# One encoder layer on one core: earlier copies of an inverse, a second bank for local products, and more planned room between a product and what it waits for

## The chip, the cores and the metric

The kernel runs on one core of a Trainium2 chip. The metric is the device time of one execution in microseconds: the median of the runs shown, and beside it one execution recorded by the hardware profiler. All times are in microseconds (us) unless marked ns.

## The reference

One layer over a prompt of 2048 tokens and a sample of 32, 1024 wide, in fp32. What matters here is the order of the stages and the chunked delta rule of mixer B.

```python
h = rmsnorm(x) * (1 + sc1) + sh1
p = h @ w_in                                  # u, v | q, k, v | z | a, b
a_out = u * (W_s @ rmsnorm(v) + b_s)          # mixer A, chunks of 128 tokens
q, k, v = l2norm(silu(causal_conv(qkv)))      # mixer B, 4 heads of 128
sol = triangular_solve(I + tril(k k^T * decay), [v * beta, k * beta * exp(gc)])
for chunk: v_new = u_i - w_i @ s
           o = qg_i @ s + attn_i @ v_new
           s = s * gl_i + kg_i^T @ v_new
x = x + gt1 * (concat(a_out, b_out) @ w_out)
h = rmsnorm(x) * (1 + sc2) + sh2
y = rmsnorm(x + gt2 * (relu(h @ w_up)^2 @ w_down))
```

## The kernel before

**Stages.** The 2080 tokens go through the mixers in two halves (`hf` 0 and 1), each in groups of 512, 384 or 288 tokens. The stages on TensorE (PE) are: `startup` (L658: the first modulation columns, the norm, and the z columns of the first group), `v_stage` (L949: mixer A's v, 260 columns a tile), the q, k, v and z columns (L882 `mixers`, L1057 `qkv_tile`), `u_stage` (L1354), `out_stage` (L1368), and then the feed-forward part (L1532) to the end. A large product is three passes with a split of each operand into a high and a low part (`BH`, `BL` and `wh`, `wl`), 8 slices of 128 deep: 24 matmul instructions fill one PSUM bank of tag `g`. The feed-forward part names its banks `f`.

**Small products beside them.** Per head and half: *local* products per pair of 128-token chunks (`delta_local`, L1094: four transposes, two products of 256 columns and two transposes, all in the bank with tag `L`), an *inverse* of a 128 x 128 triangle per chunk (`delta_inv`, L1176), and a *chain* over the chunks (`delta_chain`, L1268): per chunk and pair of heads a step of four products with the state (`pa`), a step of two with the inverse (`px`), and a step of four (`pu`), all in banks of tag `C`. Each step reads what VectorE (DVE) or ScalarE (ACT) made of the step before. Other tags are `B` (the inverse) and `M` (norms).

**The inverse.** For each head, `delta_inv` cuts 16 x 16 diagonal blocks out of `nb` and copies them to a DRAM tile `nd` with eight copies (ten in the second half), reads `nd` back as `N` with one block a partition, solves on GpSimd (POOL), writes the result to `ud_d` with two copies (four in the second half) and reads it back as `ud`. All copies are issued by SyncE's queue (SP).

**What sets the order.** Nothing runs in the order of the text. `Program.op` records each operation with its engine, an assumed duration and its predecessors. Predecessors come from the regions that operations read and write (`Mem.read`, `Mem.write`). A `View` keeps the region it had before a `re` (a rearranged view): an index taken after `re` narrows the shape, not the region. `schedule` (L245) then lays all operations out in assumed time, and each engine's program is the order of their assumed starts. At run time every engine goes through its own list strictly in that order.

In `schedule` a priority goes first (CHAIN, INV, LOCAL, EVAC, GEMM; the large products are GEMM), except that on PE small operations may be held back: while a large product is also ready, a small one is not taken until `hold` ns after it became ready (L60: `HOLD`, for LOCAL alone, 1000). An operation becomes ready when each predecessor has ended, plus an assumed latency between the engines (L272). A `bank` (L463) is taken from the ring of its tag; the next user of a bank comes after the last reader of the one before.

Of the kernel before, what the change touches and what calls it, by code (L numbers as in the profile page):

```python
# [43 lines left out]
PE, DVE, ACT, POOL, DMA, NONE = range(6)  # L44
# [5 lines left out]
LATENCY = {(PE, DVE): 230, (PE, ACT): 230, (PE, POOL): 230, (DVE, PE): 380, (DVE, DVE): 130, (DVE, ACT): 160,  # L50
           (DVE, POOL): 190, (DVE, DMA): 150, (ACT, PE): 370, (ACT, DVE): 175, (ACT, ACT): 180, (ACT, POOL): 210,
           (ACT, DMA): 150, (POOL, PE): 390, (POOL, DVE): 100, (POOL, ACT): 130, (POOL, POOL): 130, (POOL, DMA): 100}
# [4 lines left out]

CHAIN, INV, LOCAL, EVAC, GEMM, IDLE = range(6)
TURN = 84
HOLD = {LOCAL: 1000}  # L60

# [143 lines left out]
class Program:  # L207
# [37 lines left out]
    def schedule(self):  # L245

        ops = self.ops
        due = [i if o.eng == PE and o.prio == GEMM else len(ops) for i, o in enumerate(ops)]
        for i in reversed(range(len(ops))):
            due[i] = min([due[i]] + [due[j] for j in ops[i].succ])  # L250
        key = [(o.prio, due[i] if o.prio >= EVAC else i, i) for i, o in enumerate(ops)]
        free = [0.0] * 6
        port = [0.0] * 6
        wait = [[] for _ in range(6)]
        ready = [([], []) for _ in range(6)]
        table, grid, large = None, (P, P), True
        order = []

        def release(i, t):
            o = ops[i]  # L260
            if o.eng == NONE:
                finish(i, t, t)
            else:
                heapq.heappush(wait[o.eng], (t, i))

        def finish(i, start, end):
            o = ops[i]
            o.start = start
            order.append((start, i))
            for j in o.succ:  # L270
                s = ops[j]
                s.ready = max(s.ready, end + o.lat + LATENCY.get((o.eng, s.eng), 0.0))  # L272
                s.npred -= 1
                if s.npred == 0:
                    release(j, s.ready)

        for i, o in enumerate(ops):
            if o.npred == 0 and o.start == 0.0 and o.eng != NONE:
                heapq.heappush(wait[o.eng], (0.0, i))
        for i, o in enumerate(ops):  # L280
            if o.npred == 0 and o.eng == NONE and not any(k == i for _, k in order[-1:]):
                finish(i, 0.0, 0.0)
                o.npred = -1

        other = {DVE: POOL, POOL: DVE}
        while True:
            best = None
            for e in range(5):
                shared = port[other[e]] - PORT if e in other else 0.0
                t = None  # L290
                if ready[e][0]:
                    t = free[e]
                elif ready[e][1]:
                    t = max(free[e], shared)
                if wait[e]:
                    at, i = wait[e][0]
                    at = max(free[e], at, shared if ops[i].port else 0.0)
                    t = at if t is None else min(t, at)
                if t is not None and (best is None or t < best[0]):
                    best = (t, e)  # L300
            if best is None:
                break
            t, e = best
            while wait[e] and wait[e][0][0] <= t:
                i = heapq.heappop(wait[e])[1]
                heapq.heappush(ready[e][ops[i].port if e != PE else ops[i].prio == GEMM], key[i])
            shared = port[other[e]] - PORT if e in other else 0.0
            tops = [q for q in (ready[e][0], ready[e][1] if shared <= t else None) if q]
            if not tops:
                continue  # L310
            top = min(tops, key=lambda q: q[0])
            if e == PE and large and len(tops) == 2 and all(t < ops[q[-1]].ready + ops[q[-1]].hold for q in tops[0]):
                top = tops[1]
            i = heapq.heappop(top)[-1]
            o = ops[i]
            end = t + o.cost
            if e == PE:
                if o.table and o.table != grid:
                    end += 110 if o.table == (P, P) else 95
                    grid = o.table  # L320
                elif o.prio == GEMM and not large:
                    end += TURN
                large = o.prio == GEMM
            elif o.table and o.table != table:
                end += 1280
                table = o.table
            free[e] = end
            if o.port:
                port[e] = end
            finish(i, t, end)  # L330
        assert len(order) == len(ops), (len(order), len(ops))
        self.span = max(free)
        order.sort()
        return [ops[i] for _, i in order]


class Kern:
# [211 lines left out]
    def setup(self):  # L549
# [14 lines left out]
        self.nslab, self.sn = 0, None  # L564
        self.slots = [{"m": Mem(SLOT), "t": None} for _ in range(NSLOT)]
        self.bmem = [Mem(512, whole=True) for _ in range(8)]
        self.banks = {"g": [0, 1, 2], "L": [3], "C": [4, 5], "B": [6], "M": [7]}
        self.rings, self.rshape = {}, {}
        for s in range(NSLOT):
            self.era(s, F32)  # L570
# [87 lines left out]
    def startup(self):  # L658
        i, c = self.i, self.dma
        c(self.craw, i["cT"])  # L660
        self.act(self.cs, self.craw, AF.Silu)
        self.fill(self.ones, 1.0, DVE)
        self.fill(self.mhalf, -0.5, DVE)
        xr = [[8, 9, 10, 11], [4, 5, 7, 12]]
        x = [[self.slot(s, lo, (P, 512)) for s in xr[g] for lo in (0, HALF)] for g in range(2)]
        load = lambda g: [c(x[g][k], self.x_src(0)(k, 512 * g, 512)) for k in range(KT)]
        row = [self.row[:, 512 * g : 512 * g + 512] for g in range(2)]

        def stats(g):
            acc = row[g]  # L670
            self.act(acc, x[g][0], AF.Square)
            for k in range(1, KT):
                sq = self.half("E")
                self.act(sq, x[g][k], AF.Square)
                self.tt(acc, acc, sq, ALU.add, DVE if g == 0 or k % 2 else POOL)
            self.rms_row([acc], 512, acc)

        load(0)
        k1 = self.slot(13, 512, (P, 248))
        c(k1, i["k1"])  # L680
        self.adab = k1[:, :96].re("p (j k q) -> p j k q", j=6, k=KT)
        self.cp(self.nrm, k1[:, 96:120].re("p (n k) -> p n k", n=3))
        self.cp(self.ident, k1[:, 120:248])
        stats(0)
        self.sq = self.slab_list()
        self.sn = self.slab(*self.sq.pop(0))
        z = [self.next_slab(), self.sn]
        ps = [self.bank("C") for _ in range(2)]
        for e in range(2):
            self.fill(ps[e], 0.0, DVE)  # L690
        zs = [self.bank(t) for t in "gggL"]
        for k in range(KT):
            self.ada_first(k, ps[k % 2])
            self.h_tile(0, 0, k, x[0][k], row[0], self.a1, 0)
            for h in range(H):
                self.gemm_k(zs[h][:, :512], *z[h // 2], h % 2, 0, 0, k)
        for h in range(H):
            self.z_out(0, 0, h, zs[h])
        load(1)
        stats(1)  # L700
        for k in range(KT):
            self.h_tile(0, 1, k, x[1][k], row[1], self.a1, 0)
        self.next_slab()
        self.consts()
# [471 lines left out]
    def delta_inv(self, hf, h, nb):  # L1176
# [4 lines left out]
        N, U, tmp = self.new("N")[:nblk], self.new("U")[:nblk], self.new("tmp")[:nblk]  # L1181
        M = nb[:, :1024].re("p (c i) -> p c i", c=8)
        nd = self.nd_d[h][hf]
        n16 = nd[:64].re("(s c a) (j i) -> s a j c i", s=2, c=8, j=16)
        for s in range(2):
            for a in range(4):
                d = slice(32 * a + 16 * s, 32 * a + 16 * s + 16)
                self.dma(n16[s, a], M[d, :, d])
            if hf == 1:
                d = slice(1024 + 16 * s, 1040 + 16 * s)  # L1190
                self.dma(nd[64 + s].re("(j i) -> j i", j=16), nb[16 * s : 16 * s + 16, d])
# [3 lines left out]
        Uv = U.re("p (j i) -> p j i", j=16)  # L1195
# [5 lines left out]
        ud_d = self.ud_d[self.nud % 2]  # L1201
        self.nud += 1
        for s in range(2):
            d = ud_d[:8].re("c a (s j t i) -> s t (c a) j i", s=2, j=16, t=2)
            self.dma(d[s, s], Uv[32 * s : 32 * s + 32])
            if hf == 1:
                d = ud_d[8:9, 0:1].re("c a (s j t i) -> s t (c a) j i", s=2, j=16, t=2)
                self.dma(d[s, s], Uv[64 + s : 65 + s])
        ud, td = self.new("ud"), self.new("td")
        self.dma(ud[:, :nch], ud_d[:nch].re("c a (j i) -> (a j) c i", j=32))  # L1210
        tr = lambda: self.transpose32(td[:, :nch].re("p c i -> p (c i)"), ud[:, :nch].re("p c i -> p (c i)"))
# [445 lines left out]
    def put(self, ops, name, m, x):  # L1657
        ops.setdefault(name, {})[m] = self.operand(self.rp, x)
# [238 lines left out]
```

## Time and profile before

| | |
|---|---|
| median of 3 runs (lowest to highest) | 2337.24 (2336.88 to 2339.47) |
| the profiled execution | 2330.84 |
| its span, first to last instruction | 2328.8 |
| DVE busy | 1653.2 (71%) |
| ACT busy | 1226.1 (53%) |
| POOL busy | 607.5 (26%) |
| granted TensorE clock, mean | 0.998 |

The profiled execution is 6.4 below the median of the runs, and 2.0 above its own span. Busy shares are averages over stages with different limits. A matmul's record is longer than the time until the next one starts, since matmuls are pipelined: with 512 columns a record lasts about 0.39 and the next starts 0.23 later. So how late a matmul is can be seen from the distance of two starts, and only partly from the idle time that the profile gives.

### The profile page before, as it was taken

Reading aid. Unit: us, or ns where it says so; the run is one execution under the profiler, and the core shown is the slowest. Engines: PE = TensorE matmul, PEld = TensorE weight load, DVE = VectorE, ACT = ScalarE, POOL = GpSimd, SP = SyncE. Lnnn points to the kernel's source line nnn. Section 1 sums busy time; section 2 is a strip of 40 time slices with the busy share of each in tenths; the row PEclk is TensorE's granted clock in tenths of the full one; section 3 lists DMA queues with packets and bytes.
Section 4 is the critical chain, followed back from the end, with each engine's and each line's share of the span. In section 5 each row is a group of like instructions: output and inputs, shape, how many; then the busy total and the mean of one; then the engine's idle time right before and its main releaser. Section 6 shows DMA issues by size and latency. Waiting matters only on the chain.

```text
span 2328.8 us, 45703 instructions
## 1 busy us (share of the span) xinstructions
PE 2292.2 (98%) x15906; PEld 2171.0 (93%) x15906; DVE 1653.2 (71%) x3651; ACT 1226.1 (53%) x2816; POOL 607.5 (26%) x830
## 2 busy tenths in 40 slices
PE   7999999999999999999999999999999999999998
PEld 4877879999999888999999999999999999999998
DVE  5557646667655546589999989776668886666775
ACT  5465546666655435376556555753344564334343
POOL 2235331332423323345544424200000250000001
PEclk9999999999999999999999999999999999999999
DMA  9789666657557767888777786997667797666771
GB/s 322 224 291 317 222 183 214 188 166 232 165 157 225 242 204 232 262 290 277 248 255 251 256 280 229 344 321 233 221 214 252 264 302 232 221 214 215 246 225 54
DMA packets 367247, 552.59 MB, mean 237 GB/s; under 512 B 70988, under 2 KB 191200, under 8 KB 367016
## 3 DMA queue, kind: packets, MB, share of 16 engines
q1 hardware_dynamic: 367016, 549.68, 72.5%
q8 instruction: 125, 2.05, 0.4%
q14 instruction: 106, 0.87, 0.1%
HBM read 395.25 MB, written 154.28 MB: 236 GB/s over the span
## 4 chain that ended last, share of the span: by engine, by line
PE 59%; DMA 3%; DVE 2%; issue 1%; ACT 1%; POOL 0%; SPq 0%; POOLq 0%; DVEq 0%; ACTq 0%
PE f L412 52%; PE g L412 6%; DMA s<-th_d 1%; PE C L412 1%; DVE s L366 1%; DVE s L371 1%; ACT s L351 0%; DVE BL L366 0%; DMA wh<-sd_d 0%; DVE wl L366 0%; POOL s L366 0%; DMA wr<-w_o 0%; PE B L412 0%; DMA th_d<-s 0%; ACT BH L351 0%
## 5 line engine op out<-in xcount | busy, mean ns | idle before, releaser
L351 ACT ACTIVATE s<-s 128x348 fp32r<-128x348 f32 (+13 forms) x1077 | 496.0, 483 | 341.3 <-DVE s L366 131.4
L412 PE MATMUL f<-s,wh 128*128 128x348 f32 (+1 forms) x2768 | 662.4, 322 | 0.4 <-DVE s L366 0.3
L412 PEld LDWEIGHTS f<-s,wh 128*128 128x128 f32 x2768 | 481.0, 188 | 2.2 <-DVE s L366 1.9
L366 DVE TENSOR_TENSOR s<-f,s 128x348 f32<-128x348 f32 (+1 forms) x696 | 349.6, 515 | 170.4 <-PE f L412 169.2
L412 PE MATMUL f<-s,wl 128*128 128x348 f32 (+1 forms) x1384 | 444.9, 321 | 0.0
L412 PE MATMUL g<-BH,wh 128*128 128x512 f32 (+2 forms) x1112 | 411.3, 370 | 0.0
L412 PE MATMUL g<-BH,wl 128*128 128x512 f32 (+2 forms) x1112 | 391.4, 352 | 0.0
L412 PE MATMUL g<-BL,wh 128*128 128x512 f32 (+2 forms) x1112 | 390.1, 351 | 0.0
L366 DVE TENSOR_TENSOR s<-s,s 128x348 fp32r<-128x348 f32 (+7 forms) x679 | 350.9, 546 | 45.7 <-POOL s L366 16.7
L412 PE MATMUL f<-BL,wh 128*128 128x348 f32 (+1 forms) x1024 | 330.2, 322 | 0.0
L412 PE MATMUL f<-BH,wh 128*128 128x348 f32 (+1 forms) x1024 | 329.3, 322 | 0.0
L412 PE MATMUL f<-BH,wl 128*128 128x348 f32 (+1 forms) x1024 | 328.7, 321 | 0.0
L351 ACT ACTIVATE wh<-s 128x512 fp32r<-128x512 f32 (+1 forms) x277 | 173.7, 634 | 232.0 <-PE f L412 190.6
L366 POOL TENSOR_TENSOR s<-s,s 128x512 f32<-128x512 f32 (+5 forms) x156 | 197.6, 1275 | 330.5 <-ACT s L351 163.4
L366 POOL TENSOR_TENSOR s<-s 64x39 f32<-64x39 f32 (+12 forms) x298 | 159.5, 535 | 444.0 <-issue 381.7
L412 PEld LDWEIGHTS f<-s,wl 128*128 128x128 f32 x1384 | 260.6, 188 | 0.0
L366 DVE TENSOR_TENSOR wl<-s,wh 128x512 fp32r<-128x512 f32 (+1 forms) x277 | 215.4, 786 | 35.7 <-ACT wh L351 34.6
L412 PEld LDWEIGHTS g<-BH,wh 128*128 128x128 f32 x1112 | 209.6, 188 | 22.7 <-issue 5.2
L412 PEld LDWEIGHTS g<-BH,wl 128*128 128x128 f32 x1112 | 208.9, 188 | 19.1
L412 PEld LDWEIGHTS g<-BL,wh 128*128 128x128 f32 x1112 | 210.0, 189 | 16.7 <-DVE BL L366 0.2
L371 DVE SCALAR_TENSOR_TENSOR s<-s,s,s 128x256 f32<-128x256 f32 (+5 forms) x318 | 164.2, 538 | 59.4 <-ACT s L351 34.2
L366 DVE TENSOR_TENSOR wl<-wr,wh 128x512 fp32r<-128x512 f32 (+2 forms) x164 | 159.1, 973 | 57.5 <-ACT wh L351 54.9
(116 smaller groups left out, 3328.0 us busy)
## 6 DMA issues: line engine op xcount, KB each, us to landing
s<-w_u SPq DMA_DIRECT2D x124, 256.0 KB
s<-w_d SPq DMA_DIRECT2D x121, 256.0 KB
wh<-su_d SPq DMA_DIRECT2D x114, 256.0 KB
wl<-su_d SPq DMA_DIRECT2D x114, 256.0 KB
wh<-sd_d SPq DMA_DIRECT2D x100, 256.0 KB
wl<-sd_d SPq DMA_DIRECT2D x100, 256.0 KB
wr<-w_b SPq DMA_DIRECT2D x42, 512.0 KB
s<-adaw SPq DMA_DIRECT2D x32, 512.0 KB
```

The source lines that it names most:

```text
L351: self.p.op(ACT, c, lambda: nc.scalar.activation(out=R(out), in_=R(in_), func=func, **{k: R(v) for k, v in kw.items()}), [out, accum], [in ...
L366: self.p.op(eng, c, lambda: e.tensor_tensor(out=R(out), in0=R(a), in1=R(b), op=op), [out], [a, b])
L371: self.p.op(DVE, c, lambda: nc.vector.scalar_tensor_tensor(out=R(out), in0=R(a), scalar=R(s), in1=R(b), op0=op0, op1=op1), [out], [a, s, b])
L412: nc.tensor.matmul(R(out), R(l), R(r), **kw)
```

## The change

Four things are changed.

1. `SLACK`: in the planner, a PE operation that is not a large product and that follows one on another engine (or a DMA) is taken to be ready 300 ns later than before.
2. `HOLD` now also holds CHAIN and INV products back, for 300 ns, while a large product is ready.
3. Bank 2 moves from tag `g` to tag `L`: large products of the mixers have two banks in turn instead of three, local products two instead of one. In `startup` the four z tiles take two `g` and two `L` banks.
4. The copies into `nd` and `ud_d` move the same bytes, but each is now written as a slice of the rows it writes, rearranged afterwards. Its region is then those rows alone, and the eight copies no longer count as writers of one another's region.

No operation is added or removed. ACT loads its function tables 37 times in the new order instead of 40.

```diff
 CHAIN, INV, LOCAL, EVAC, GEMM, IDLE = range(6)
 TURN = 84
-HOLD = {LOCAL: 1000}
+SLACK = 300
+HOLD = {CHAIN: 300, INV: 300, LOCAL: 1000}
...
                 s = ops[j]
-                s.ready = max(s.ready, end + o.lat + LATENCY.get((o.eng, s.eng), 0.0))
+                slack = SLACK if s.eng == PE != o.eng and s.prio < GEMM else 0.0
+                s.ready = max(s.ready, end + o.lat + LATENCY.get((o.eng, s.eng), 0.0) + slack)
...
-        self.banks = {"g": [0, 1, 2], "L": [3], "C": [4, 5], "B": [6], "M": [7]}
+        self.banks = {"g": [0, 1], "L": [3, 2], "C": [4, 5], "B": [6], "M": [7]}
...
-        zs = [self.bank(t) for t in "gggL"]
+        zs = [self.bank(t) for t in "ggLL"]
...
         nd = self.nd_d[h][hf]
-        n16 = nd[:64].re("(s c a) (j i) -> s a j c i", s=2, c=8, j=16)
         for s in range(2):
             for a in range(4):
                 d = slice(32 * a + 16 * s, 32 * a + 16 * s + 16)
-                self.dma(n16[s, a], M[d, :, d])
+                self.dma(nd[32 * s + a : 32 * s + 32 : 4].re("c (j i) -> j c i", j=16), M[d, :, d])
...
         for s in range(2):
-            d = ud_d[:8].re("c a (s j t i) -> s t (c a) j i", s=2, j=16, t=2)
-            self.dma(d[s, s], Uv[32 * s : 32 * s + 32])
+            put = lambda d, v: self.dma(d[:, :, 512 * s : 512 * s + 512].re("c a (j t i) -> t (c a) j i", j=16, t=2)[s], v)
+            put(ud_d[:8], Uv[32 * s : 32 * s + 32])
             if hf == 1:
-                d = ud_d[8:9, 0:1].re("c a (s j t i) -> s t (c a) j i", s=2, j=16, t=2)
-                self.dma(d[s, s], Uv[64 + s : 65 + s])
+                put(ud_d[8:9, 0:1], Uv[64 + s : 65 + s])
```

The change reorders every engine's list up to the feed-forward part. From the first `f` product on, PE's list differs in 69 of 8164 instructions. Three places follow on which the prediction rests. Rows name the line, the operation, output and inputs (`s` are SBUF slots, numbers after an underscore are tile numbers), the output's size, and how often the row stands.

**SP, the copies of the first head's blocks into `nd`.** Before, the last three of the eight and the read of `N`:

```order
L404 DMA nd_d_0_163<-s_493 16x8x16
L404 DMA v_d_103<-s_489 128x512
L404 DMA s_476<-kq_d_98 128x2x256
L404 DMA nd_d_0_163<-s_493 16x8x16
L404 DMA s_477<-v_d_102 128x256
L404 DMA pk_d_1_121<-s_475 128x768
L404 DMA kq_d_100<-s_489 128x512
L404 DMA nd_d_0_163<-s_493 16x8x16
L404 DMA s_495<-pk_d_1_121 128x768
L404 DMA s_472<-nd_d_0_163 64x256
```

and with the change all eight:

```order
L406 DMA s_490<-h_d_160 128x384
L406 DMA nd_d_0_163<-s_493 16x8x16 x8
L406 DMA pk_d_3_114<-s_475 128x768
L406 DMA s_477<-v_d_102 128x256
L406 DMA s_476<-kq_d_98 128x2x256
L406 DMA kq_d_99<-s_489 128x512
L406 DMA s_472<-nd_d_0_163 64x256
```

The eight copies stood with two to four other DMAs between each two of them; now they stand in one run, and four DMAs later comes the read of `N`.

**PE, one step of the chain in the second half, in `out_stage`.** `C` rows of `s_482` are the products with the inverse and the state update, `g` rows the large product. Before:

```order
L412 MATMUL C_10104<-s_482,s_470 128x128
L412 MATMUL g_9989<-BH_71,wh 128x512
L412 MATMUL g_9989<-BL_79,wh 128x512
L412 MATMUL g_9989<-BH_71,wl 128x512
L412 MATMUL g_9989<-BH_72,wh 128x512
L412 MATMUL g_9989<-BL_80,wh 128x512
L412 MATMUL g_9989<-BH_72,wl 128x512
L412 MATMUL C_10100<-s_482,s_469 128x128 x2
L412 MATMUL C_10100<-s_482,s_470 128x128 x2
```

and with the change:

```order
L414 MATMUL C_9861<-s_482,s_470 128x128
L414 MATMUL g_9773<-BH_77,wh 128x512
L414 MATMUL g_9773<-BL_85,wh 128x512
L414 MATMUL g_9773<-BH_77,wl 128x512
L414 MATMUL g_9773<-BH_78,wh 128x512
L414 MATMUL g_9773<-BL_86,wh 128x512
L414 MATMUL g_9773<-BH_78,wl 128x512
L414 MATMUL g_9824<-BH_71,wh 128x512
L414 MATMUL g_9824<-BL_79,wh 128x512
L414 MATMUL g_9824<-BH_71,wl 128x512
L414 MATMUL C_9855<-s_482,s_469 128x128 x2
L414 MATMUL C_9855<-s_482,s_470 128x128 x2
```

Six large matmuls stood between the two steps, now nine. In the step ahead of these rows it was six and is twelve.

**PE, local products of the first half, in the q, k, v columns.** `L` rows of `ident` are transposes. Before:

```order
L423 MATMUL L_2732<-ident,s_477 128x128 x2
L412 MATMUL g_2572<-BH_78,wh 128x512
L412 MATMUL g_2572<-BL_86,wh 128x512
L412 MATMUL g_2572<-BH_78,wl 128x512
L412 MATMUL g_2643<-BH_71,wh 128x512
L412 MATMUL g_2643<-BL_79,wh 128x512
L412 MATMUL g_2643<-BH_71,wl 128x512
L412 MATMUL g_2643<-BH_72,wh 128x512
L412 MATMUL g_2643<-BL_80,wh 128x512
L412 MATMUL g_2643<-BH_72,wl 128x512
L423 MATMUL L_2748<-ident,s_476 128x128 x4
```

and with the change:

```order
L425 MATMUL L_2651<-ident,s_477 128x128 x2
L425 MATMUL L_2657<-ident,s_476 128x128 x4
L414 MATMUL g_2578<-BH_75,wh 128x512
L414 MATMUL g_2578<-BL_83,wh 128x512
L414 MATMUL g_2578<-BH_75,wl 128x512
L414 MATMUL g_2578<-BH_76,wh 128x512
L414 MATMUL g_2578<-BL_84,wh 128x512
L414 MATMUL g_2578<-BH_76,wl 128x512
```

The last transposes of one pair of chunks and the first of the next used to be apart, since they shared a bank that had to be read first; now they stand together, in two banks.

## The prediction

> **What bounds the kernel now.** The page gives the span; the view of windows cuts it at the end of startup (100), at the first feed-forward products (1015) and before the tail (2290). Columns: length, busy time and count of PE, PEld, DVE, ACT and POOL, then granted clock, DMA share and GB/s.
>
> ```profile
> span 2328.8 us, 45703 instructions
> 0.00:100.00 100.00, 83.78 (x606) 62.60 (x607) 57.75 (x136) 49.41 (x96) 24.97 (x38) 1.00 0.83 278
> 100.00:1015.00 915.00, 905.78 (x7120) 810.51 (x7119) 557.34 (x1546) 503.35 (x1324) 300.00 (x576) 1.00 0.71 224
> 1015.00:2290.00 1275.00, 1273.29 (x7994) 1269.22 (x7993) 1018.33 (x1928) 663.60 (x1377) 271.07 (x204) 1.00 0.75 249
> 2290.00:2329.00 39.00, 29.39 (x192) 28.63 (x190) 19.81 (x44) 9.72 (x20) 11.47 (x12) 0.90 0.20 73
> ```
>
> PE is the bound nearly everywhere: it is idle for 1.7 us in the 1275 of the feed-forward part, whose list the change hardly touches, and for 9.2 in the 915 of the mixers, where the moved work stands. The clock is full there. So the change can win only what PE loses between 100 and 1015, and can lose what it makes PE wait there or in startup.
>
> The idle time understates that loss, since records overlap. PE's timeline shows it at one chain step, and at the first and the last late one (start, length, operation, idle before it):
>
> ```profile
> 400.32 0.60 PE L423 MATMUL L<-ident,s 128*128 128x128 f32 x4
> 401.20 0.49 PE L412 MATMUL C<-s,s 128*128 128x128 f32 x2 [0.28 <-DVE s L371]
> ...
> 851.42 0.40 PE L412 MATMUL g<-BH,wl 128*128 128x512 f32 x1
> 852.09 0.71 PE L412 MATMUL C<-s,s 128*128 128x128 f32 x4 [0.27 <-DVE s L371]
> ...
> 853.79 0.40 PE L412 MATMUL g<-BH,wl 128*128 128x512 f32 x1
> 854.03 1.05 PE L412 MATMUL C<-s,s 128*128 128x128 f32 x8
> ...
> 906.23 0.60 PE L423 MATMUL M<-ident,rcol 128*128 128x128 f32 x4
> 906.76 0.71 PE L412 MATMUL C<-s,s 128*128 128x128 f32 x4
> ```
>
> At 854.03 the step starts 0.24 after the large matmul ahead of it, the usual distance (0.23). At 852.09 it starts 0.67 after: 0.44 late, of which the profile calls 0.27 idle. PE goes strictly through its list, so every large product behind waits too. Read so, by the distance of starts, 42 of the 340 chain products between 100 and 1015 begin more than 0.06 late, the first at 401.20 (0.44), the last at 906.76 (0.09), none by more than 0.50; together 7.9 us. The same reading gives 2.8 for the inverse (4 products), 4.7 for the norms and gates (18), 3.9 for the local products (25) and 0.7 for the transposes behind the chain. That is 20.0 us, all that can be won here. The view of waits names what ended the longest of them:
>
> ```profile
> PE C L412 <- DVE s L371: 2.1, 8, 0.3
> PE M L423 <- POOL rcol L366: 1.3, 2, 0.8
> PE B L412 <- issue: 1.3, 1, 1.3
> PE M L412 <- POOL s L366: 1.0, 3, 0.4
> PE B L412 <- DVE s L397: 0.8, 1, 0.8
> PE L L423 <- DMA s<-kq_d: 0.3, 1, 0.3
> ```
>
> **The later plan for small products.** SLACK and HOLD put 300 and 300 ns more between a chain or inverse product and what it waits for, as planned time filled with large products; norms get 300, local products 300 on top of their hold. The order bears this out: of the chain steps, the median has 12 large matmuls between it and the step before, where it was 6, and the fewest are 3, where it was none. Six matmuls of 0.17 to 0.23 are 1.0 to 1.4 us. The largest lateness of a chain product, 0.50, is below that, so if DVE and ACT were as late as now, all 7.9 would go. Not all of it will: the engines ahead run in order too, and one table load on ACT costs 1.28 (row below), more than the slack. I take 6.5 off; bounds 3 (only what is under 0.2 late each goes) and 7.9. The norms' five long waits (0.4 to 1.0 by the same reading) shrink by 0.3 each: 1.5 off, bounds 0 and 4.7. Local products: half of the 3.9 are distances of 0.09 to 0.11 inside a group that is just starting, which no order removes; 1.0 off, bounds 0 and 3.9. The transposes behind the chain: 0.3 off, bounds 0 and 0.7. The inverse waits for a landing:
>
> ```profile
> 801.87 4.73 DMA s<-ud_d
> 806.62 0.49 DVE s L397
> 807.16 0.74 PE B L412 x55
> ```
>
> The chain of waits shows `ud` landing 4.73 after its issue at 801.87; the planner assumes 3.5 for the latency, so 0.3 of slack does not cover it, while 0.6 covers half. 0.8 off, bounds 0 and 2.8.
>
> The added wait delays the chain itself: 102 steps by 0.6 are up to 61 us of planned time. Queued behind a held product on PE are only large ones that need nothing of it; what waits for the chain's end is `out_stage` of the second half, through `mix_d`. By the order the chain ends earlier all the same, with 3486 large matmuls ahead of its last product and not 3588, because each inverse is ready earlier. That costs nothing while large products last, which the 9.2 us of idle in 915 show.
>
> **The copies.** SP's timeline for the first head, and its row for all of them:
>
> ```profile
> 251.33 0.34 SPq L404 DMA_DIRECT2D nd_d<-s  x1
> ...
> 277.49 0.55 SPq L404 DMA_DIRECT2D nd_d<-s  x1
> ...
> 280.05 0.49 SPq L404 DMA_DIRECT2D s<-nd_d  x1
> L404 SPq DMA_DIRECT2D nd_d<-s x72: 318/430/1288, 251.3 to 766.9; - x72
> ```
>
> The eight copies took from 251.33 to the read at 280.05, 28.7 us. In one run they are 8 x 0.43 = 3.4 us of SP plus a landing (the 4.73 above is one): about 8, so each inverse comes some 20 us sooner. PE is not waiting for it, apart from the 2.8 counted, so I take 0 for the gain. The loads that now stand behind eight copies are up to 3.4 later; the only wait of PE for such a load is 0.3 (`kq_d` above), once per head that is 0 to 2.4. I take 0, as the loads keep their places relative to each other.
>
> **Fewer visits to small products.** PE leaves the large products 241 times in the new order, 265 in the old. It is worth nothing, as two and four transposes show:
>
> ```profile
> 252.06 0.39 PE L412 MATMUL g<-BH,wl 128*128 128x512 f32 x1
> 252.29 0.38 PE L423 MATMUL L<-ident,s 128*128 128x128 f32 x2
> ...
> 252.74 0.40 PE L412 MATMUL g<-BL,wh 128*128 128x512 f32 x1
> ...
> 254.36 0.40 PE L412 MATMUL g<-BH,wl 128*128 128x512 f32 x1
> 254.60 0.60 PE L423 MATMUL L<-ident,s 128*128 128x128 f32 x4
> ...
> 255.27 0.39 PE L412 MATMUL g<-BL,wh 128*128 128x512 f32 x1
> ```
>
> From the large matmul ahead to the second one behind there are 0.68 and 0.91; less two distances of 0.23 that leaves 0.22 and 0.45, twice as much for twice the transposes. A visit has no price of its own: 0, bounds -0.5 and +0.5 (24 visits by the 0.02 that the rows leave open).
>
> **Two banks for large products.** A bank must now be read out while the next tile fills: 24 matmuls, 5.6 us at 512 columns, 4.2 at 384, 2.9 at 260. From the end of a tile's last matmul to the end of its last reader, the 173 tiles took 1.06 in the median and under 2.9 in nine of ten. Three took longer than the next tile's filling, by 2.8 together. One read by ACT is 0.49 in the median; what comes before it in ACT's list makes the rest, as for a tile whose last matmul started at 138.06:
>
> ```profile
> L351 ACT ACTIVATE s<-g x133: 357/490/646, 53.7 to 795.6; 128x384 f32<-128x384 f32 x40, 128x512 f32<-128x512 f32 x39, 128x256 f32<-128x256 f32 x32, 128x288 f32<-128x288 f32 x20
> ...
> 142.67 1.28 ACT L351 ACT_TABLE_LOAD   x1
> 143.97 0.60 ACT L351 ACTIVATE s<-g 128x512 f32<-128x512 f32 x1
> ```
>
> With three banks this was hidden. I take 2.0 on: the three stay late, ACT loads three tables fewer. Bounds: 0, if readers move up, and 7.4, if every release comes 1 us later (then 8 tiles are late). The Trainium skill, Perfetto Trace Analysis, section Matmuls, wants independent groups rotated through different PSUM banks, so that reading one overlaps the next group. Two banks still do that; by the trace the third was needed three times.
>
> **Startup.** One load of half a weight slab, of the size in this row of the DMA list, now stands ahead of later modulation loads on SP:
>
> ```profile
> wr<-w_b SPq DMA_DIRECT2D x42, 512.0 KB
> ```
>
> At startup's 278 GB/s that is 1.9 us. PE may wait so much longer at 22, or less later on: 0, bounds -1.9 and +1.9.
>
> **The sum:** -6.5 - 1.5 - 1.0 - 0.3 - 0.8 + 2.0 = -8.1, so about -8 against the profiled 2330.84, which would give 2322.8. That execution lies 6.4 under the median of the runs; the change should move both alike, and 2337.24 - 8 is 2329.
>
> **The rivals.**
> - *The late steps stay late.* They are late since DVE and ACT are, in order and behind table loads, and the new plan moves both. For it: 1.28 against 0.6 of slack. Against it: no chain product is over 0.50 late. Then only 3 of the chain and 1 of the rest go, and 3 to 4 come on for banks: 2337. Here the change does not do what it says.
> - *Two banks run dry.* ACT reads tiles behind chain, inverse and local work; with one bank less its queue decides. By the 173 releases: 2.8 on as they are, 12.7 if each comes 1.5 later (13 tiles), 20.6 at 2 later (20 tiles). From about 1.6 later it outweighs the 10 saved. At 2 later the time is 2337.24 - 10.1 + 20.6 = 2348. Against it: ACT is busy 503 of 915 and the planner knows of the two banks. The Trainium skill's rule above speaks of this case.
> - *Everything goes.* Earlier inverses take the landings out of the way as well and releases move up: the 20 without the distances inside groups, 18 off: 2319.
>
> **How the numbers follow.** About 0.2% (4.7 us) is what a measurement of this kernel can tell from no change. The forecast, 2324 to 2332.5, gets 0.53; everything goes, 0.12; late steps stay late, 0.22; banks run dry, 0.13. So faster 0.65, same 0.22, slower 0.13. The range, 2319 to 2340, leaves out most of the bank case and the best ends of the third.
>
> **What would show it.** Right: chain products after 100 start at the usual distance, their lateness under 2 in sum; PE's idle in the mixers falls to 4 to 6; `nd` copies of a head stand within 4 us of each other; the feed-forward part keeps its length. Wrong: PE `g` waiting for an ACT or DVE read of `g` several times, a longer startup, or chain products late by as much as now behind a table load.

## The result and the profile after

| | before | after |
|---|---|---|
| median of 7 runs (lowest to highest) | 2338.47 (2336.88 to 2345.42) | 2331.56 (2327.49 to 2333.06) |
| the profiled execution | 2330.84 | 2328.48 |
| its span | 2328.8 | 2326.5 |

The ratio is 0.9964 (95% interval 0.9953 to 0.9976): faster by 6.9 in the medians. The profiled executions are only 2.4 apart. Before's, 2330.84, lies under every other time on record for that kernel (the lowest is 2333.26), so the two profiles show less than the runs do. The change's profile is 3.1 under its own median. What is read from one profile below holds for that execution; from one to the next it can differ by some us.

The windows of the changed kernel, cut as before (length, busy time and count of PE, PEld, DVE, ACT, POOL, then clock, DMA share, GB/s):

```profile
0.00:100.00 100.00, 82.90 (x580) 61.86 (x582) 58.58 (x135) 49.51 (x94) 23.97 (x38) 0.97 0.78 264
100.00:1015.00 915.00, 906.59 (x7160) 816.45 (x7157) 561.42 (x1549) 497.97 (x1327) 296.75 (x576) 1.00 0.71 226
1015.00:2290.00 1275.00, 1273.41 (x7997) 1269.63 (x7996) 1018.85 (x1927) 662.83 (x1376) 272.38 (x205) 1.00 0.75 248
2290.00:2329.00 39.00, 26.83 (x175) 26.07 (x173) 18.81 (x41) 8.38 (x17) 10.54 (x11) 0.86 0.20 73
```

In the first 100 us PE did less (580 instructions, before 606) at a lower granted clock (0.97, before 1.00). Between 100 and 1015 it did more (7160, before 7120), though its idle time hardly fell: 8.4 after 9.2. The feed-forward part takes 1308.2 from its first product to the end of PE's list, before 1308.3. So the gain of the profiled pair is in the mixers, some 6, less 3.8 in startup (the 200th large product starts at 74.1, before at 70.3).

Read by the distance of starts, as in the prediction, the lateness between 100 and 1015 is now: chain 2.4 (6 products late, before 42), inverse 0 (before 2.8), norms and gates 2.3 (4.7), local products 5.7 (3.9), transposes 0.4 (0.7): 10.9 in sum, before 20.0. The view of PE's waits in the same stretch (what PE waited for; us in total, times, longest):

```profile
PE g L414 <- ACT s L353: 3.0, 3, 1.4
PE L L425 <- DVE s L373: 1.7, 1, 1.7
PE C L414 <- DVE s L373: 1.6, 3, 0.7
PE M L425 <- POOL rcol L368: 0.8, 1, 0.8
```

The first row is new: large products that wait for a bank to be read. One of its two long waits in the timeline, PE and ACT:

```profile
106.76 1.28 ACT L353 ACT_TABLE_LOAD   x1
...
108.33 1.28 ACT L353 ACT_TABLE_LOAD   x1
...
109.62 0.66 ACT L353 ACTIVATE s<-g 128x256 f32<-128x256 f32 x2
...
110.06 0.39 PE L414 MATMUL g<-wh,BH 128*128 128x260 f32 x1 [1.40 <-ACT s L353]
```

The v tiles of mixer A fill a bank in 24 x 0.12 = 2.9. ACT loads two tables, 2.56, before it reads the tile. With two banks PE stands 1.56 by distances; the same happens once more at 458.04 (1.58). SP's timeline has the eight copies of a head in one row now:

```profile
257.22 3.64 SPq L406 DMA_DIRECT2D nd_d<-s  x8
...
263.31 0.49 SPq L406 DMA_DIRECT2D s<-nd_d  x1
```

From the first copy to the read of `N` are 6.1, where it was 28.7.

### The profile page after: what moved, and what is told of

It reads as the page before. It is cut to its first block, busy times and chain, and to the rows that moved or that the text cites. A ratio compares the mean times of both kernels' runs of the same rounds, so it can differ in the third digit from the quotient of the medians.

```text
span 2326.5 us, 45701 instructions
## 1 busy us (share of the span) xinstructions
PE 2289.7 (98%) x15906; PEld 2174.0 (93%) x15906; DVE 1657.7 (71%) x3651; ACT 1218.7 (52%) x2813; POOL 603.6 (26%) x830
## 4 chain that ended last, share of the span: by engine, by line
PE 86%; DMA 5%; DVE 4%; ACT 2%; issue 1%; POOL 1%; SPq 0%; POOLq 0%; DVEq 0%; ACTq 0%
PE f L414 51%; PE g L414 26%; PE C L414 3%; PE B L414 2%; DVE s L368 1%; PE L L414 1%; ACT s L353 1%; DVE s L373 1%; PE M L414 1%; POOL s L368 1%; PE L L425 1%; DMA s<-th_d 1%; DMA s<-ada 1%; DVE BL L368 1%; DMA s<-xT 1%
## 5 line engine op out<-in xcount | busy, mean ns | idle before, releaser
L353 ACT ACTIVATE s<-s 128x348 fp32r<-128x348 f32 (+14 forms) x1077 | 494.5, 482 | 325.3 <-DVE s L368 125.4
L414 PE MATMUL g<-BH,wh 128*128 128x384 f32 (+2 forms) x1104 | 407.7, 369 | 0.2 <-ACT s L353 0.2
L368 DVE TENSOR_TENSOR s<-s,s 128x348 fp32r<-128x348 f32 (+8 forms) x679 | 349.1, 542 | 55.6 <-ACT s L353 26.0
L414 PE MATMUL g<-BH,wl 128*128 128x384 f32 (+2 forms) x1104 | 388.7, 352 | 0.0
L414 PE MATMUL g<-BL,wh 128*128 128x384 f32 (+2 forms) x1104 | 387.2, 351 | 0.0
L353 ACT ACTIVATE wh<-wr 128x512 fp32r<-128x512 f32 (+2 forms) x164 | 130.3, 795 | 130.5 <-PE f L414 57.3
```

The costliest lines, as they stand in the source:

```text
L353: self.p.op(ACT, c, lambda: nc.scalar.activation(out=R(out), in_=R(in_), func=func, **{k: R(v) for k, v in kw.items()}), [out, accum], [in ...
L368: self.p.op(eng, c, lambda: e.tensor_tensor(out=R(out), in0=R(a), in1=R(b), op=op), [out], [a, b])
L414: nc.tensor.matmul(R(out), R(l), R(r), **kw)
```

## The experiments

Twelve kernels ran, each beside before on the same chip. *Lateness* is the sum over small products from 100 us to the first feed-forward product, as above; it leaves out the modulation's products in bank `B`, whose waits stand as `DMA s<-adaw` in the views. *g stalls* are distances ahead of a large product that are over 0.22 too long. Both come from one profiled execution each. In the column "plan", 300 is SLACK and HOLD as in the change, SLACK or HOLD is that half alone, and "later" leaves startup out. Medians and ratios come from 4 to 12 runs a kernel, with 21 to 32 of before (medians 2338.38 to 2338.95). The ratio is not the quotient of the two medians, but that quotient lies inside its interval every time.

| kernel | plan | g, L banks | new copies | median | ratio (95%) | lateness | g stalls |
|---|---|---|---|---|---|---|---|
| before | - | 3, 1 | no | 2338.47 | 1 | 20.0 | 1.0 |
| plan_only | 300 | 3, 1 | no | 2340.54 | 1.0008 (0.9998-1.0018) | 10.0 | 8.1 |
| banks_only | - | 2, 2 | no | 2341.25 | 1.0013 (1.0002-1.0024) | 18.6 | 3.6 |
| copies_only | - | 3, 1 | yes | 2335.02 | 0.9991 (0.9981-1.0000) | 23.4 | 0 |
| no_banks | 300 | 3, 1 | yes | 2341.77 | 1.0011 (1.0001-1.0022) | 18.7 | 0.3 |
| no_plan | - | 2, 2 | yes | 2344.46 | 1.0027 (1.0014-1.0039) | 22.4 | 3.1 |
| no_copies | 300 | 2, 2 | no | 2330.65 | 0.9959 (0.9947-0.9971) | 10.7 | 3.1 |
| the change | 300 | 2, 2 | yes | 2331.56 | 0.9964 (0.9953-0.9976) | 10.9 | 3.5 |
| one_L_bank | 300 | 2, 1 | yes | 2332.11 | 0.9959 (0.9946-0.9971) | 14.8 | 3.8 |
| v_three_banks | 300 | 2 (v: 3), 2 | yes | 2331.66 | 0.9961 (0.9949-0.9974) | 15.0 | 0.8 |
| no_slack_in_startup | 300 later | 2, 2 | yes | 2329.97 | 0.9964 (0.9952-0.9977) | 15.3 | 3.0 |
| slack_without_hold | SLACK | 2, 2 | yes | 2334.05 | 0.9977 (0.9968-0.9986) | 18.4 | 3.4 |
| hold_without_slack | HOLD | 2, 2 | yes | 2337.99 | 0.9995 (0.9986-1.0005) | 17.0 | 3.1 |
| slack_600 | SLACK 600 | 2, 2 | yes | 2321.59 | 0.9918 (0.9905-0.9932) | 5.0 | 2.3 |

The theory at the start: the planned room is the gain, two `g` banks give part of it back, the copies change little. Rival A: the early copies are the gain. Rival B: the second `L` bank is.

### The plan alone

```diff
-HOLD = {LOCAL: 1000}
+SLACK = 300
+HOLD = {CHAIN: 300, INV: 300, LOCAL: 1000}
```

The line of `schedule` that adds SLACK goes with it; the rest is as before.

> Before with SLACK and HOLD of the change, but its own three g banks, one L bank and old copies. Theory (the gain is the planned room, two banks give part of it back): chain lateness under 2.5 us in sum (before 7.9), no PE stall of 1.4 for an ACT read of g at 110 or 458, startup as long as in the change; 7 to 11 us below before, so 1 to 4 below the change. Rival A (the gain is the early copies): within 2 us of before, the inverse still late. Rival B (the second L bank frees PE): at most 3 us below before.

The lateness halved (10.0; the chain's is 2.8, a little over the 2.5 expected), much as the theory says, but the time did not follow: 2340.54, and its interval includes no change. The first row of its waits shows where it went:

```profile
PE g L414 <- ACT BH L353: 5.4, 1, 5.4
```

and its timeline (PE, SP and ACT) why:

```profile
943.68 0.38 PE L425 MATMUL C<-ident,s 128*128 128x128 f32 x2
...
944.26 0.80 SPq L406 DMA_DIRECT2D mix_d<-s  x2
...
947.56 1.09 SPq L406 DMA_DIRECT2D s<-mix_d  x2
...
950.51 0.78 ACT L353 ACTIVATE BH<-s 128x288 fp32r<-128x288 f32 x2 [1.58 <-DMA s<-mix_d]
...
951.01 0.61 PE L414 MATMUL g<-BH,wh 128*128 128x288 f32 x1 [5.36 <-ACT BH L353]
```

The last product of the chain comes at 943.68; its result goes to DRAM and back, and the next large product in PE's list needs it: 5.36 of idle. By the order that last product stands behind 3771 large ones, before behind 3627, in the change behind 3513. (The count goes up to this transpose; the prediction's 3588 and 3486 go up to the last product with the state.) The held chain ends too late when nothing else brings it forward. The wait costs more than itself, as the windows around it show:

```profile
943.00:950.90 7.90, 2.65 (x16) 2.29 (x14) 3.02 (x7) 2.16 (x5) 0.92 (x2) 0.90 0.60 182
950.90:956.00 5.10, 4.88 (x16) 4.36 (x17) 3.44 (x9) 2.77 (x7) 0.93 (x1) 0.50 0.86 290
956.00:962.00 6.00, 6.00 (x35) 6.00 (x35) 3.38 (x6) 2.91 (x5) 2.50 (x2) 0.99 0.78 261
```

The clock column is 0.50 for the 5.1 behind the wait: some 2.5 more, by estimate. There is a second loss, in startup: 563 PE instructions in the first 100 us (580 in the change), and the 350th large product starts at 102.2 (98.1 in the change), with a norm product in a wait of its own:

```profile
81.93 2.22 PE L414 MATMUL M<-s,s 128*128 128x128 f32 x8 [2.30 <-DVE s L373]
```

### The banks alone, the copies alone

```diff
-        self.banks = {"g": [0, 1, 2], "L": [3], "C": [4, 5], "B": [6], "M": [7]}
+        self.banks = {"g": [0, 1], "L": [3, 2], "C": [4, 5], "B": [6], "M": [7]}
```

Startup's z tiles take their banks as in the change.

> Before with only the banks changed (two g, two L). Theory (two banks are too few where ACT loads two tables in v_stage): chain lateness still 6 to 9 us, PE stalls of over 1 us for an ACT read of g in v_stage, 2 to 5 us above before. Rival B (the second L bank is the gain): 3 to 6 us below before. Rival A: within 2 us of before.

2341.25, in the theory's range, with chain lateness 8.1 and two g stalls of 1.59 and 1.38 in `v_stage`. Rival B falls.

The second kernel has only the new declarations of `nd` and `ud_d`.

> Before with only the copies declared by rows. Theory: chain lateness still 6 to 9 us, the inverse's 2.8 us of lateness under 1; 0 to 3 us below before. Rival A (early copies are the gain): 6 us or more below before.

2335.02, 3.9 under before in the medians and 0 to 4.4 by the interval. The theory's part on lateness failed: the inverse is as late as before (2.6, where under 1 was expected), the chain at 10.1, over the range. Rival A's 6 is out of the interval. What the gain of this kernel is made of was not settled: its lateness is higher than before's.

### The change without its banks, copies or plan

> The change with before's banks (three g, one L). Theory (room pays as long as the chain ends early enough; two g banks cost the two stalls of 1.6 us in v_stage): by the order the last chain product stands behind 3663 large ones (change 3513, before 3627, the run with the plan alone 3771, where PE then waited 5.4 us for BH), at least 52 ahead of its reader, so no wait of PE for BH over 1 us; the v_stage stalls gone; 1 to 4 us below the change. Rival (the second L bank is what makes room for the chain): a wait of over 2 us for BH at 930 to 955, 1 us or more above the change.

> The change with the old copies. Theory (the copies only bring the chain's end forward; with the second L bank it stands behind 3588 large products, early enough): chain lateness under 3 us, no wait for BH over 1 us, 0 to 4 us above the change. Rival A (the early copies carry the gain): 5 us or more above the change.

> The change without SLACK and HOLD: banks and copies alone. Theory (the room takes the lateness away): chain lateness 6 to 11 us, 4 to 9 us above the change, within 3 us of before. Rivals A and B (copies or the second L bank carry the gain): within 2 us of the change.

`no_copies` is as fast as the change, though its copies stand apart again: the theory holds and rival A falls. `no_plan` is 12.9 slower than the change, with chain lateness 12.0; lateness and g stalls together make 11.1 of it in the two profiles. All of this is more than the theory gave: new banks and copies without the room lose 6.1 against before. `no_banks` refutes the theory: no wait for BH, as expected, but 10.2 slower than the change instead of 1 to 4 faster. Its rival gave that time, but by a wait for BH that is not there. So plan and banks do not add up. Against the runs of before beside them, the plan alone is 1.6 slower (its interval includes no change), the banks alone 2.3, and both together (`no_copies`) win 7.7. With the new copies it is the same: 3.9 faster without plan and banks, 3.4 slower with the plan alone (`no_banks`), 6.1 slower with the banks alone (`no_plan`).

Part of it shows in the first 100 us. `no_banks` has the same wait of a norm product at 82.67 (2.29) as the plan alone, and the two have the fewest PE instructions there. The windows row of the plan alone:

```profile
0.00:100.00 100.00, 81.94 (x563) 58.70 (x564) 58.59 (x134) 48.85 (x91) 25.11 (x38) 0.95 0.78 266
```

and of `no_banks`:

```profile
0.00:100.00 100.00, 81.11 (x559) 58.35 (x559) 58.68 (x134) 48.81 (x91) 25.13 (x38) 0.95 0.77 264
```

Their 350th large product starts at 102.2 and 103.0, in the change at 98.1, in before at 97.1. So with SLACK and three `g` banks startup came out longer in both profiles, by 4 to 5. In `no_banks` the clock also fell to half for 3.4 at 677 and at 927, behind waits of an inverse product (2.10 idle) and a norm product (1.01). That profile is of a run 3 slower than the kernel's median.

The granted clock, however, is on record for every run. It averages 0.9948 over the 12 runs of the plan alone and 0.9943 over the 11 of `no_banks`, 0.9964 over the change's, and 0.9961 to 0.9972 over those of every other kernel. So the lower clock belongs to the plan with three banks, and not to one execution; 0.002 of 2330 is 4.7, by this estimate about half of the 10.2. `no_plan`, at 0.9966, is slow without it. Why the plan makes PE wait so with three banks stays open.

### Which bank it is

> The change with bank 2 left idle after startup: two g banks and one L bank. Theory (the second L bank is what lets the planned room pay, since local products then overlap two reads and need no dense stretch of PE): 6 us or more above the change, at or above before; lateness from 100 to the first feed-forward product 4 us or more above the change's. Rival (planning with two g banks is the partner, the second L bank does nothing): within 2 us of the change. A wait for BH is not expected, the last chain product stands behind 3621 large ones.

```diff
-        self.banks = {"g": [0, 1], "L": [3, 2], "C": [4, 5], "B": [6], "M": [7]}
+        self.banks = {"g": [0, 1], "L": [3], "z": [2], "C": [4, 5], "B": [6], "M": [7]}
```

Startup takes its fourth z tile from `z`. The theory that the second `L` bank is the partner fell: 2332.11, as the change. The partner of the plan is that large products are planned with two banks; what local products have does not show in the time. Lateness is 3.9 above the change's all the same, just under the theory's 4.

### A third bank in v_stage, startup without SLACK

```diff
-        self.banks = {"g": [0, 1], "L": [3, 2], "C": [4, 5], "B": [6], "M": [7]}
+        self.banks = {"g": [0, 1], "L": [3, 2], "v": [0, 1, 2], "C": [4, 5], "B": [6], "M": [7]}
...
-        ps = self.bank("g")
+        ps = self.bank("v")
```

The second line is in `v_tile`.

> The change, with bank 2 lent to the v tiles of mixer A, so that v_stage has three banks in turn as before, and everything else two. Theory (v_stage is where two banks are too few): no PE stall over 1 us for an ACT read of g at 110 and 458, 2 to 4 us below the change. Rival (the stalls are taken up by later slack or come back elsewhere): within 1 us of the change.

The stalls are gone from the waits:

```profile
PE B L414 <- DVE s L399: 2.5, 2, 1.7
PE C L414 <- DVE s L373: 1.7, 4, 0.9
PE B L414 <- DMA s<-adaw: 1.6, 1, 1.6
PE B L414 <- DVE s L382: 1.3, 1, 1.3
```

No row for `g` behind ACT; in their place the inverse is late by 5.1 (the change 0). The time is the same, which is the rival. That the stalls came back elsewhere, its second half, fits this profile but is not shown: it is of a run 3.3 over its median. The time says as well that it is not the v tiles that need two banks.

```diff
-                slack = SLACK if s.eng == PE != o.eng and s.prio < GEMM else 0.0
+                slack = SLACK if s.eng == PE != o.eng and s.prio < GEMM and j >= self.past else 0.0
```

`past` is the number of operations recorded when `startup` is through.

> The change, but SLACK counts only for operations recorded after startup, so that startup has its old order on PE. Theory (the later transposes of the modulation make startup longer: the 200th large product starts at 74.1 where it was 70.3): 200th large product at 70 to 71.5, 2.5 to 4.5 us below the change, 9 to 12 below before. Rival (startup's length is only the clock's chance, a half-speed window more or less from one execution to the next): within 1 us of the change.

The rival holds: 200th large product at 74.8, the ratio equal to the change's. Startup's length differs by that much between executions of one order, as `copies_only` shows with before's own order of PE there (200th large product at 73.8, before 70.3). The window from 20 to 30 of `copies_only`:

```profile
20.00:30.00 10.00, 6.66 (x39) 2.95 (x35) 7.59 (x17) 3.09 (x5) 2.56 (x3) 0.68 0.89 348
```

and of before:

```profile
20.00:30.00 10.00, 7.98 (x61) 3.70 (x61) 9.62 (x25) 4.68 (x8) 3.12 (x6) 1.00 0.96 379
```

Same order, 39 instructions instead of 61, at a clock of 0.68. PE first waited 2.83 for a modulation load, up to 24.64, in before 1.37, up to 22.76. Of the 13 other profiles, 12 have stretches at half clock between 20 and 100, 3.4 to 10.2 in sum. Before's profile has none. By estimate that is worth 1.7 to 5.1, so part of what it lies under its median.

Three kernels with the change's time show lateness of 14.8 to 15.3 where the change shows 10.9. Two of these profiles are 3.3 and 3.5 above their kernel's median, the change's 3.1 under. So a difference of 4 in lateness between two profiles can belong to the executions and not to the kernels.

### How much room, and which half of it

> The change without HOLD for chain and inverse, SLACK alone. Theory (lateness decides, and 300 of room covers some 60 per cent of the steps that were late): chain lateness 2 to 6 us, 1 to 5 us above the change. Rival (a visit to small products has a price of about 0.5 us: the four kernels near 2331 have 225 to 227 visits, those at 2335 to 2344 have 243 to 255): with 244 visits 7 us or more above the change, whatever the lateness.

> The change without SLACK, HOLD for chain and inverse alone. Theory: chain and inverse as with half the room, norms as late as before; chain lateness 2 to 6 us, 1 to 5 us above the change. Rival (price of a visit): with 238 visits 5 to 7 us above the change.

Both fall between `no_plan` and the change: SLACK alone is 2.5 above it, in the theory's range, HOLD alone 6.4, over it and in the rival's (chain lateness 6.5 and 7.3, both over the range). The rival still falls: SLACK alone with its 244 visits should have been 7 or more above, and `one_L_bank` has 241 visits and the time of the change, which has 227 (counted as before has 251; the prediction's count, 241 and 265, gives the same difference of 24). HOLD is simply the weaker half.

> The change with SLACK 600 instead of 300. Theory (what is left late are single steps and groups of local products just starting, and two bank stalls, which no room removes): chain lateness under 2 us, within 2 us of the change. Rival (lateness falls on with room): 3 us or more below the change.

2321.59: the rival. It is 10.0 below the change, and the fastest of all. Lateness fell to 5.0, the local products from 5.7 to 1.8, the norms from 2.3 to 1.0, the chain from 2.4 to 1.4; with the g stalls that is 7.1 of the 10.0. Its waits from 100 to 1015:

```profile
PE g L414 <- ACT s L353: 1.4, 1, 1.4
PE B L414 <- DMA s<-adaw: 1.3, 1, 1.3
PE g L414 <- DVE wl L368: 0.5, 1, 0.5
PE M L414 <- POOL s L368: 0.4, 1, 0.4
```

and its window there:

```profile
100.00:1015.00 915.00, 911.21 (x7208) 824.18 (x7207) 569.24 (x1563) 505.65 (x1345) 312.23 (x583) 1.00 0.72 229
```

PE is idle for 3.8 there (the change 8.4), and no chain or local product stands in the list of waits. The last transpose behind the chain stands behind 3588 large products, still early enough. More than 600 was not tried.

## Why the prediction was right, and where it was not

**The time.** 2329 was forecast and 2331.56 measured, in the forecast's own 2324 to 2332.5; -8.1 against -6.9. Of the signs that it named, the copies of a head (3.64 apart, under 4) and the length of the feed-forward part came true. Two did not: the chain's lateness is 2.4, not under 2, and PE's idle in the mixers 8.4, not 4 to 6. And a sign of being wrong is there, PE waiting three times for a read of `g`.

**The later plan.** Right in kind: `no_plan` is at 2344, HOLD, SLACK, both and SLACK 600 take it down to 2338, 2334, 2332 and 2322. By terms, after against before in the two profiles: chain -5.5 (forecast -6.5), inverse -2.8 (-0.8), norms -2.4 (-1.5), local +1.8 (-1.0), transposes -0.3 (-0.3). The sum is -9.2, forecast -10.1. The argument "the largest lateness of a chain product, 0.50, is below that, so if DVE and ACT were as late as now, all 7.9 would go" was too simple. A new order makes other steps late. One chain product of the change, whose large neighbour starts at the usual 0.12 behind the one ahead of it:

```profile
401.27 0.28 PE L414 MATMUL g<-wh,BL 128*128 128x260 f32 x1
401.39 0.28 PE L414 MATMUL g<-wl,BH 128*128 128x260 f32 x1
402.36 1.16 PE L414 MATMUL C<-s,s 128*128 128x128 f32 x8 [0.68 <-DVE s L373]
```

It is 0.84 late, more than any before. And the local term, half of which "no order removes", went to 1.8 with SLACK 600.

**The chain's end.** The prediction put no price on the longer chain, since by the order it "ends earlier all the same", for the reason that "each inverse is ready earlier". In the change it does cost nothing. The reason was incomplete: without the copies but with the banks it also ends early enough (3588); without both it does not (3771), and that price is the 5.36 and the half clock behind it. The earlier inverse is part of the cause (3513 with the copies), the banks the other.

**The copies.** 0 was right beside the plan and the banks: `no_copies` against the change is 0.9 the other way. Alone they gave 3.9, unexplained. **Visits**: the price of 0 held.

**Two banks for large products.** This is the step that failed: "I take 2.0 on". As a term of the profile it was nearly right: g stalls 3.5 after 1.0, at a tile read behind table loads, as the prediction had shown for 138.06. But it was priced as a cost that adds to the others. Alone the banks cost 2.3; with the room, taking the third `g` bank away gains 10 (`no_banks` to the change, and `one_L_bank`). The plan's -10.1 has the same fault: it was read from a trace with three banks and holds for two (`no_plan` to the change, -12.9), while with three the plan gains nothing (1.6 the other way). The two faults cancel in the sum: that it came within 1.2 of the measured gain is luck in this part.

**Startup.** 0 was right in the runs (`no_slack_in_startup`), though the two profiles differ by 3.8.

**The rivals.** "The late steps stay late" fell: the chain's lateness went from 7.9 to 2.4. "Two banks run dry" stopped at two stalls of 1.6. "Everything goes", 18 off, is not what the change did, but SLACK 600 comes to 17 off.

## What to carry to other kernels

Where engines run lists that were laid out ahead, lateness of small steps on the bound engine was won here by more planned room between a step and its input. The limit seen is a longest dependent chain that ends too late for its reader. Try the size of that room first: here 600 gave 10 more than 300. Try such edits together as well as one by one: plan and banks each gained nothing alone and won together.

## What the runs showed of the hardware

A wait of PE can cost more than its length. In the kernel without SLACK in startup, a norm product waits 2.59 for POOL, and then (PE's timeline):

```profile
189.76 1.13 PE L414 MATMUL M<-ones,s 128*128 128x1 f32 x6 [2.59 <-POOL s L368]
...
191.32 0.63 PE L414 MATMUL g<-BL,wh 128*128 128x512 f32 x1
191.75 0.63 PE L414 MATMUL g<-BH,wl 128*128 128x512 f32 x1
...
193.73 0.40 PE L414 MATMUL g<-BL,wh 128*128 128x512 f32 x1
193.97 0.39 PE L414 MATMUL g<-BH,wl 128*128 128x512 f32 x1
```

The large products behind it start 0.43 apart until 193.46, and 0.24 to 0.27 from there. The records give a granted clock of 0.5 for 3.4 there, so the wait costs about 1.7 more, by estimate. Half clock followed waits of 5.36 and 2.59, and in the same kernel one of 1.24 at 403.51; the change's waits of 1.4 at 110.06 and 458.04 had none behind them. Between 100 and 1015 the 14 profiles hold 44 waits of PE of 1 us or more. With each of the four longest (1.93, 2.10, 2.59 and 5.36) half clock began in the wait or within 3.5 us of its end; of the 40 others, 1.01 to 1.72, that is so for five. What decides among the shorter ones is not shown. The Trainium skill, TensorE: Matmul & The Clock Gate, section HAM oscillation, asks that PE not idle for more than about 3.4 us. The 5.36 agrees; the 2.59 and the 1.24 are shorter, and here the measurement decides.
